# A boundary on eight single PSUM banks, with the next stage's first block product issued inside it

## The chip, the cores and the metric

The kernel runs on one core of a Trainium2 chip. The metric is device time in microseconds of one execution. Engines are called by their work: TensorE multiplies matrices and transposes, VectorE and ScalarE work element by element and read PSUM, GpSimd works on SBUF alone, and SyncE issues the DMAs. The profile's short names are PE, DVE, ACT, POOL and SP.

## The reference

A decoder trunk of two layers over 1024 positions and 1024 channels. A layer has two sub-layers; each is a layer norm of `alpha * x + (1 + gate) * f(x * (1 + scale) + shift)`, with shift, scale and gate from a conditioning vector. The first `f` is a token mixer (a convolution module, differential attention and a spatial gating unit side by side, then one output projection), the second a convolutional feed-forward network:

```python
def conv_ffn(h, w_up, b_up, conv_w, conv_b, w_down, b_down):
    up = causal_dwconv(h @ w_up + b_up, conv_w, conv_b)
    g, val = jnp.split(up, 2, axis=-1)
    return (jax.nn.silu(g) * val) @ w_down + b_down

for l in range(DEPTH):
    ...
    y = jnp.concatenate([y_a, y_b, y_c], axis=-1) @ w_out[l] + b_out[l]
    x = layer_norm(DEEPNORM_ALPHA * x + (1.0 + g1) * y, ln_g[l, 0], ln_b[l, 0])
    h = x * (1.0 + sc2) + sh2
    y = conv_ffn(h, w_up[l], b_up[l], conv_f_w[l], conv_f_b[l], w_down[l], b_down[l])
    x = layer_norm(DEEPNORM_ALPHA * x + (1.0 + g2) * y, ln_g[l, 1], ln_b[l, 1])
```

All is float32. The output projection, the layer norm behind it and the start of `h @ w_up` are the place of this change.

## The kernel before

Positions are held in eight row tiles of 128 (`NT` = 8), channels in eight column tiles of 128. A float32 operand of a matrix product is split into a high part in the matrix format (a ScalarE cast) and a low part (a subtraction, mostly on VectorE); `mm3` (lines 128 to 132) multiplies high by high, high by low and low by high, three matmuls of 128x128 by 128x512 for one product.

*The output projection.* `stage3` (line 891) first runs `out_fill` (line 852), which adds the products of the first head groups into the residual rows `r[t]`, one PSUM bank of 512 columns at a time. Then it opens a new PSUM pool with `self.psum(3, 2)` (three pairs of banks under the name `mm`, two single banks under the name `bank`) and loads and splits the first weights of the up-projection (`up_first`). `boundary` with w = 0 (line 915) runs `out_group` (line 874) for the last two heads: for each row tile, in the order 4, 5, 6, 7, 0, 1, 2, 3, it fills one pair of banks `og` with twelve matmuls and adds its 1024 columns to `r[t]` in one VectorE instruction (line 887).

*The norm and the transposes.* After each row tile `after(t)` runs `ln_rows` (line 348): statistics on VectorE (lines 352, 354, 137), a power on GpSimd (line 138), and the normalisation on ScalarE for tiles 4 to 7 (line 361) or on VectorE for tiles 0 to 3 (line 363); the row is also written to memory. When the later half of the positions (tiles 4 to 7) is normalised, `comb_early` transposes it; when the earlier half (0 to 3) is, `comb_late` does the rest. (In code and text "half" 1 is tiles 4 to 7, and half 0, tiles 0 to 3, comes second in time.) `comb_in` (line 954) takes a bank `tr`, puts four transposes into it, one from each row tile, and has ScalarE scale and shift them into SBUF (line 958). `comb_split` (line 960) casts on ScalarE and subtracts on VectorE (line 962); `tt` in `comb_late` (line 979) adds and subtracts the blocks.

*The up-projection.* `up_phase` (line 1087) multiplies 2x2 blocks with seven products in place of eight; `product(ps, H, n)` (line 1077) is the n-th of them, four blocks k of three matmuls each, from the splits `B11`, `B21`, `B22`, `T1` to `T4` that the boundary made. Product 3 uses `B22` (the later half alone), 1 and 2 use `B11` and `B21` (the earlier half alone), 5, 6, 7 and 4 use `T1`, `T2`, `T3` and `T4`. It is a loop over 22 feature tiles, written out by hand. In the first pass the order on TensorE is 3, 1, 2, 5, 6, 7, then 1 of the next tile, then 4. Product 6 accumulates into the bank of product 1, behind the ScalarE copy `e1` of it (line 1127); product 7 likewise behind the copy `u2` (line 1176). `e1` lies in a page of the tag `Rb`, which has four pages; the boundary's blocks `f` have held all four.

*What sets the order.* Outside `up_phase` a planner orders each engine's queue when the kernel is built: an instruction goes out by its place in the program once its inputs and its tile's memory are free in the planner's own time. Inside `up_phase` the order of TensorE, ScalarE and VectorE is that of the program text. On the chip each queue runs in the order it was given.

Of the kernel before, what the change touches and what calls it, by code (L numbers as in the profile page):

```python
# [17 lines left out]
ALU = mybir.AluOpType  # L18
# [32 lines left out]
class Trunk:  # L51
# [822 lines left out]
    def out_group(self, lhs, w, r, after=None, tiles=range(NT), new=False):  # L874
        nc = self.nc
        for t in tiles:
            ts_ = slice(t * P, (t + 1) * P)
            ps = self.mm("og")
            for n in range(2):
                ns = slice(n * 512, (n + 1) * 512)  # L880
                for k in range(len(lhs)):
                    self.mm3(ps[:, ns], lhs[k][0][:, ts_], lhs[k][1][:, ts_], w[k][0][:, ns], w[k][1][:, ns], k == 0,
                             k == len(lhs) - 1)
            if new:
                nc.scalar.copy(r[t], ps)  # L885
            else:
                nc.vector.tensor_tensor(out=r[t], in0=ps, in1=r[t], op=ALU.add)  # L887
            if after:
                after(t)

    def stage3(self, l, H, O, att):
        nc = self.nc
        att, grow = att
        raws = self.page(H + "a", "wout", shape=(P, 4, 1024))
        for i in range(4 - len(self.woA)):
            self.woA.append(self.scaled_wout(l, KA[len(self.woA)], grow, raws[:, i]))
        wA = [self.split_wout(O, raw) for raw in self.woA]
        ab = None
        if l == 0:
            ab = self.page("rows", "ab")  # L900
            nc.sync.dma_start(ab, self.gab(0, 0, 1))
        order = (4, 5, 0, 1, 2, 3, 6, 7)
        r = {}
        for t in order:
            next(att)
            r[t] = self.load_res(t, ab)
        for _ in att:
            pass
        self.out_fill(self.lhsA, wA, r, order, 1.0 if l else ALPHA)
        self.out_fill(self.lhs0, self.wB[:2], r, order)  # L910
        self.psum(3, 2)
        self.up_first(l, O + "c")
        return r, self.lhsB, self.wB[2:]

# [58 lines left out]
    def comb_late(self, r, H, sc, sh):  # L973
        nc = self.nc
        f = self.parts("Rb", 2, F32) + self.parts("Rb", 2, F32)
        f1, f2, f22 = H["f12"], H["f3"], H["f22"]

        def tt(o, x, y, op):
            nc.vector.tensor_tensor(out=o, in0=x, in1=y, op=op)
        for k in range(4):  # L980
            self.comb_split(H["B22"], k, f22[k], nc.vector)
        for q in range(4):
            self.comb_in(r, 0, q, sc, sh, f[q])
        for q in range(4):
            self.comb_split(H["B11"], q, f[q], nc.vector)
        for q in range(4, 8):
            self.comb_in(r, 0, q, sc, sh, f[q])
        for q in range(4, 8):
            self.comb_split(H["B21"], q - 4, f[q], nc.vector)
        for k in range(4):  # L990
            tt(f2[k], f22[k], f1[k], ALU.subtract)
            tt(f1[k], f1[k], f[k], ALU.subtract)
            self.comb_split(H["T1"], k, f1[k], nc.vector)
        for k in range(4):
            tt(f[k], f2[k], f[k], ALU.add)
            tt(f[4 + k], f[4 + k], f[k], ALU.subtract)
            self.comb_split(H["T2"], k, f[k], nc.vector)
        for k in range(4):
            self.comb_split(H["T3"], k, f2[k], nc.vector)
        for k in range(4):  # L1000
            self.comb_split(H["T4"], k, f[4 + k], nc.vector)
# [85 lines left out]
    def up_phase(self, l, H, A):  # L1087
        nc = self.nc
# [32 lines left out]
                                       in1=u[:, d:], op0=ALU.mult, op1=ALU.add)  # L1121
            tt(u[:, 0:2], u[:, 0:2], self.ffcorr[:, m, :])

        b, d = self.bank("upb"), self.bank("upd")
        self.product(d, H, 3)
        self.product(b, H, 1)
        act.copy(e1, b)
        n11 = n12 = n21 = n22 = o11 = None
        for f in range(NF + 1):
            run, nxt = f < NF, f + 1 < NF  # L1130
            if nxt:
                o22 = n22 if f else None
                k = 2 * ((f + 1) % 2)
# [20 lines left out]
            if run:  # L1154
                d3, d = d, self.bank("upd")
# [45 lines left out]
            if nxt:  # L1201
                b = nb
# [35 lines left out]
    def ffn(self, l, H, A, O):  # L1238
        nc = self.nc
        self.ffn_cols(l)  # L1240
        self.psum(0, 8)
        with self.tc.manual_schedule(engines={nc.tensor.engine, nc.scalar.engine, nc.vector.engine}):
            self.up_phase(l, H, A)
        self.psum(3, 2)
        pages = lambda tag, n: [self.page(tag, "dn", F32R) for _ in range(n)]
        ya, xc = pages(A + "a", 8), pages(O + "c", 4)
        xa = []
        for _ in range(2):
            t = self.page(O + "a", "dn", F32R, (P, 4, 1024))
            xa += [t[:, i] for i in range(4)]  # L1250
        yb, yc = pages(A + "b", 4), pages(A + "c", 4)
        xb = []
        for _ in range(2):
            t = self.page(O + "b", "dn", F32R, (P, 2, 1024))
            xb += [t[:, i] for i in range(2)]
        sets = [(xa[:6], xa[6:] + yb), (ya[:6], yc + ya[6:])]
        grow = self.gate_row(l, 1)
        r = {}
        f0 = 0
        sizes = (2, 3, 3, 3, 3, 3, 2, 3)  # L1260
        for j, n in enumerate(sizes):
            last = j == len(sizes) - 1
            acts, wts = (xb, xc) if j == 0 else sets[j % 2]
            lhs = [self.load_act(l, f0 + i, acts[2 * i], acts[2 * i + 1]) for i in range(n)]
            w = [self.load_wdown(l, f0 + i, wts[2 * i], wts[2 * i + 1], grow) for i in range(n)]
            f0 += n
            if j == 0:
                for t in (4, 5, 6, 7, 0, 1, 2, 3):
                    r[t] = self.page("Ra" if t < 4 else "Rb", "r")
                self.out_group(lhs, w, r, None, (4, 5, 6, 7, 0, 1, 2, 3), True)  # L1270
                self.bg.append(self.residual_in(l, r, O))
                if l + 1 < L:
                    self.mod_tile = [self.page(O + "c", "wada") for _ in range(3)] + [self.page(O + "c", "macc")]
                    self.pump(2)
            elif not last:
                self.out_group(lhs, w, r)
                self.pump(3 * n if l + 1 < L else 2)
            else:
                self.drain_bg()
                if l + 1 < L:  # L1280
                    for ww in range(2):
                        self.affine_cols(l + 1, ww)
                    pre = self.za_first(l + 1, A)
                    Hn = self.boundary(l, 1, lhs, w, r, O)
                    self.bg.append(self.residual(l, r, "tmp"))
                    return Hn, pre
                self.final_rows(l, lhs, w, r)
# [143 lines left out]
```

## Time and profile before

| what | value |
|---|---|
| time, median of 3 runs (lowest to highest) | 2440.98 us (2439.22 to 2441.18) |
| the profiled execution's own time | 2437.79 us |
| its span, first to last instruction | 2436.1 us |
| TensorE busy | 2308.1 us (95%) |
| VectorE busy | 1956.1 us (80%) |
| ScalarE busy | 1049.9 us (43%) |
| granted TensorE clock, mean | 0.974 |
| 1024-column additions of line 887 | 128, mean 1218 ns |

The profile is one execution. Busy time counts an instruction from its start to its end, and successive ones on an engine overlap by a tenth of a microsecond or so; where they queue, the distance from start to start is what one costs. In a row of an engine's order, the bracket is the idle time ahead of it and what ended that. The first layer's boundary lies from about 507 to 571 us of the span and the second's 1201 us later, from about 1708 to 1772.

### The profile page before, as it was taken

To read this page: it belongs to the slowest core of one execution; us is meant where nothing else is said; L and a number is where in the kernel's file an instruction comes from. 1 tells how busy PE (TensorE), PEld (TensorE's weight loads), DVE (VectorE), ACT (ScalarE), POOL (GpSimd) and SP (SyncE) were. 2 spreads that over 40 slices of the span, in tenths; PEclk is the share of its full clock that TensorE was granted. 3 is DMA by queue.
4 is the path that set the end of the run, shared out by engine and by line. 5 is a ranking of instruction groups with operands and counts; after the bars stand their busy time and mean duration, and the time that the engine had idled before them with its cause. 6 is when DMAs were issued, how large, how long until landed. Compare 5 with 4: busy or idle time off the path is not lost.

```text
span 2436.1 us, 28260 instructions
## 1 busy us (share of the span) xinstructions
PE 2308.1 (95%) x10846; PEld 1886.4 (77%) x10846; DVE 1956.1 (80%) x2650; ACT 1049.9 (43%) x1692; POOL 328.9 (13%) x165
## 2 busy tenths in 40 slices
PE   8998999979999999999959999999899999999996
PEld 7787778767888887788848877777688888878885
DVE  7898876778887888877978988657987777797857
ACT  4214754646554555311130257555654555561111
POOL 1143260410000000000020541214100000000003
PEclk9998999999999999999979999999999999999998
DMA  7433462122332333745523244320232222254301
GB/s 294 156 116 120 140 224 104 61 95 90 110 113 88 112 113 121 263 141 179 190 70 117 78 143 160 130 95 27 99 100 87 78 78 87 87 176 169 122 26 69
DMA packets 87672, 294.06 MB, mean 121 GB/s; under 512 B 9265, under 2 KB 18801, under 8 KB 86001
## 3 DMA queue, kind: packets, MB, share of 16 engines
q1 hardware_dynamic: 87536, 292.26, 35.4%
q8 instruction: 85, 1.39, 0.2%
q14 instruction: 51, 0.41, 0.1%
HBM read 228.23 MB, written 64.00 MB: 120 GB/s over the span
## 4 chain that ended last, share of the span: by engine, by line
PE 67%; DVE 17%; issue 6%; ACT 4%; DMA 3%; POOL 2%; SPq 0%; POOLq 0%; DVEq 0%; ACTq 0%
PE upb L1083 6%; PE upb L1084 6%; PE upb L1085 6%; PE og L130 5%; PE og L131 5%; PE og L132 5%; PE sc L733 3%; PE upd L1084 3%; PE upd L1085 3%; PE upd L1083 3%; DVE convacc L410 2%; PE pv L778 2%; PE of L130 2%; PE of L132 2%; PE of L131 2%
## 5 line engine op out<-in xcount | busy, mean ns | idle before, releaser
L1083 PE MATMUL upb<-comb,uw 128*128 128x512 f32 x704 | 274.9, 391 | 9.9 <-DVE upc L1107 5.0
L130 PE MATMUL og<-dn,dn 128*128 128x512 f32 x704 | 275.3, 391 | 2.6 <-ACT r L885 2.1
L131 PE MATMUL og<-dn,dn 128*128 128x512 f32 x704 | 274.5, 390 | 0.0
L132 PE MATMUL og<-dn,dn 128*128 128x512 f32 x704 | 274.3, 390 | 0.0
L1084 PE MATMUL upb<-comb,uw 128*128 128x512 f32 x704 | 274.0, 389 | 0.0
L1085 PE MATMUL upb<-comb,uw 128*128 128x512 f32 x704 | 273.9, 389 | 0.0
L1107 DVE TENSOR_TENSOR uw<-wu,uw 128x512 fp32r<-128x512 f32 x210 | 144.1, 686 | 125.3 <-ACT uw L1110 125.3
L1120 DVE SCALAR_TENSOR_TENSOR cv<-upc,pc,cv 128x1023 f32<-128x1023 f32 (+1 forms) x176 | 225.4, 1280 | 2.9
L138 POOL TENSOR_TENSOR lnrs<-lnrs,mhalf 128x1 f32<-128x1 f32 x32 | 24.8, 779 | 1421.4 <-DVE lnrs L137 1414.9
L887 DVE TENSOR_TENSOR r<-og,r 128x1024 f32<-128x1024 f32 x128 | 155.7, 1218 | 59.0 <-PE og L132 58.4
L410 DVE SCALAR_TENSOR_TENSOR convacc<-convy,pc,convacc 128x1023 f32<-128x1023 f32 (+14 forms) x120 | 176.2, 1469 | 2.3
L125 ACT CAST dn<-actr 128x1024 fp32r<-128x1024 f32 x44 | 46.1, 1049 | 298.1 <-issue 224.4
L1083 PEld LDWEIGHTS upb<-comb,uw 128*128 128x128 f32 x704 | 132.1, 188 | 41.0 <-DVE upc L1107 6.7
L1110 ACT CAST uw<-wu 128x512 fp32r<-128x512 f32 x210 | 121.7, 616 | 83.6 <-DVE wu L1107 77.1
L130 PEld LDWEIGHTS og<-dn,dn 128*128 128x128 f32 x704 | 132.2, 188 | 31.5 <-ACT r L885 3.4
L1085 PEld LDWEIGHTS upb<-comb,uw 128*128 128x128 f32 x704 | 132.2, 188 | 27.5
L132 PEld LDWEIGHTS og<-dn,dn 128*128 128x128 f32 x704 | 132.2, 188 | 27.4
L1084 PEld LDWEIGHTS upb<-comb,uw 128*128 128x128 f32 x704 | 132.2, 188 | 27.2
L131 PEld LDWEIGHTS og<-dn,dn 128*128 128x128 f32 x704 | 132.2, 188 | 26.8
L1083 PE MATMUL upd<-comb,uw 128*128 128x512 f32 x352 | 137.3, 390 | 0.0
L1085 PE MATMUL upd<-comb,uw 128*128 128x512 f32 x352 | 136.9, 389 | 0.0
L1084 PE MATMUL upd<-comb,uw 128*128 128x512 f32 x352 | 136.9, 389 | 0.0
(312 smaller groups left out, 5474.4 us busy)
## 6 DMA issues: line engine op xcount, KB each, us to landing
wada<-in_w_ada SPq DMA_DIRECT2D x96, 512.0 KB, 4.6
wu<-in_w_up_t SPq DMA_DIRECT2D x84, 512.0 KB, 3.6
d_act<-cv SPq DMA_DIRECT2D x44, 512.0 KB, 2.6
actr<-d_act SPq DMA_DIRECT2D x44, 512.0 KB, 4.6
wdn<-in_w_down SPq DMA_DIRECT2D x44, 512.0 KB, 4.2
win<-in_w_fm SPq DMA_DIRECT2D x24, 512.0 KB, 4.0
wtm<-in_w_tm SPq DMA_DIRECT2D x16, 512.0 KB, 3.7
wout<-in_w_out SPq DMA_DIRECT2D x16, 512.0 KB, 6.2
```

Of the source, the lines that this page charges most:

```text
L130: mm(ps, lh, rh, start=first, stop=False)
L131: mm(ps, lh, rl, start=False, stop=False)
L132: mm(ps, ll, rh, start=False, stop=last)
L410: nc.vector.scalar_tensor_tensor(out=acc[:, d:], in0=y[:, :S - d], scalar=w(30 - d), in1=acc[:, d:], op0=ALU.mult, op1=ALU.add)
L733: nc.tensor.matmul(ps[m][:, c0:c1], q[ms, isl], k[ms, c0:c1], start=n == 0, stop=n == 2 and c1 != w)
L887: nc.vector.tensor_tensor(out=r[t], in0=ps, in1=r[t], op=ALU.add)
L1083: mm(ps, w[:, 0, ks], hi[k], start=k == 0 and not more, stop=False, skip_group_check=True)
L1084: mm(ps, w[:, 0, ks], lo[k], start=False, stop=False, skip_group_check=True)
L1085: mm(ps, w[:, 1, ks], hi[k], start=False, stop=k == 3, skip_group_check=True)
L1107: v.tensor_tensor(out=o, in0=x, in1=y, op=op)
L1110: act.copy(self.up_w[n][:, 0], src)
L1120: v.scalar_tensor_tensor(out=u[:, d:], in0=c[:, :S - d], scalar=self.ffw[:, 2 - d, m:m + 1], in1=u[:, d:], op0=ALU.mult, op1=ALU.add)
```

## The change

Three edits. `stage3` opens the pool as eight single banks, `self.psum(0, 8)`, and the feed-forward stage no longer opens one of its own, so that row tiles, transposes and the up-projection's first products draw on the same eight banks. `out_group`, where the pool has no pairs, takes a single bank per half of a row tile and adds it to `r[t]` by itself: two VectorE instructions of 512 columns in place of one of 1024. And `comb_late` takes the bank `upd` and issues product 3 behind the splits of `B22` and ahead of the earlier half's `comb_in` calls, that is, ahead of the transposes that come second in time; `up_phase` uses that bank and no longer issues product 3 itself. The other callers of `out_group` run on pools with pairs and are as before.

```diff
@@ out_group
-            ps = self.mm("og")
+            ps = self.mm("og") if self.psb["mm"] else None
             for n in range(2):
                 ns = slice(n * 512, (n + 1) * 512)
+                po = self.bank("og") if ps is None else ps[:, ns]
                 for k in range(len(lhs)):
-                    self.mm3(ps[:, ns], lhs[k][0][:, ts_], lhs[k][1][:, ts_], w[k][0][:, ns], w[k][1][:, ns], k == 0,
+                    self.mm3(po, lhs[k][0][:, ts_], lhs[k][1][:, ts_], w[k][0][:, ns], w[k][1][:, ns], k == 0,
                              k == len(lhs) - 1)
-            if new:
+                if ps is None:
+                    nc.vector.tensor_tensor(out=r[t][:, ns], in0=po, in1=r[t][:, ns], op=ALU.add)
+            if ps is None:
+                pass
+            elif new:
                 nc.scalar.copy(r[t], ps)
             else:
                 nc.vector.tensor_tensor(out=r[t], in0=ps, in1=r[t], op=ALU.add)
@@ stage3
-        self.psum(3, 2)
+        self.psum(0, 8)
         self.up_first(l, O + "c")
@@ comb_late
         for k in range(4):
             self.comb_split(H["B22"], k, f22[k], nc.vector)
+        self.up_d = self.bank("upd")
+        self.product(self.up_d, H, 3)
         for q in range(4):
             self.comb_in(r, 0, q, sc, sh, f[q])
@@ up_phase
-        b, d = self.bank("upb"), self.bank("upd")
-        self.product(d, H, 3)
+        b, d = self.bank("upb"), self.up_d
         self.product(b, H, 1)
@@ ffn
         self.ffn_cols(l)
-        self.psum(0, 8)
         with self.tc.manual_schedule(engines={nc.tensor.engine, nc.scalar.engine, nc.vector.engine}):
             self.up_phase(l, H, A)
```

## The prediction

> **What bounds the kernel now.** I read the table of stretches first, around the first layer's boundary, to see which engine has no room there; then the order of time on each engine, to see what each waits for; then the chain of waits. Columns of the table: length, then busy time of TensorE, its weight loads, VectorE, ScalarE, GpSimd, with instruction counts, then granted TensorE clock and DMA.
>
> ```profile
> core 0: us, PE busy (x) PEld busy (x) DVE busy (x) ACT busy (x) POOL busy (x), PEclk, DMA share, GB/s
> 510.00:530.00 20.00, 19.97 (x92) 16.19 (x90) 19.30 (x39) 6.05 (x6) 3.27 (x6) 1.00 0.40 156
> 530.00:549.30 19.30, 11.31 (x57) 8.21 (x57) 18.86 (x35) 17.26 (x29) 3.52 (x2) 0.74 0.40 137
> 549.30:560.30 11.00, 11.00 (x50) 9.01 (x48) 11.00 (x20) 9.44 (x19) 0.00 (x0) 0.99 0.00 0
> 560.30:571.20 10.90, 9.07 (x39) 6.64 (x37) 10.87 (x19) 6.37 (x11) 0.00 (x0) 1.00 0.44 147
> 571.20:593.00 21.80, 21.80 (x96) 18.08 (x97) 17.65 (x25) 11.53 (x17) 0.00 (x0) 1.00 0.31 97
> 1711.20:1772.30 61.10, 50.48 (x232) 38.95 (x230) 59.93 (x109) 38.85 (x62) 6.79 (x8) 0.94 0.28 103
> ```
>
> Five rows tell it. From 510.0 to 571.2 VectorE idles 0.70 + 0.44 + 0.00 + 0.03 = 1.17 us of 61.2, while TensorE idles 8 us in the second row alone. From 571.2 on TensorE is full and VectorE has room (17.65 of 21.80). The second layer's boundary, in the last row, is the same: 61.10 - 59.93 = 1.17 us idle. So a boundary is a stretch of VectorE work of 61 us, and TensorE gets its pace back when VectorE has done it. Now TensorE's order of time:
>
> ```profile
> 507.06 0.39 PE L130 MATMUL og<-woh,ybh 128*128 128x512 f32 x1
> ...
> 522.48 0.38 PE L957 MATMUL tr<-ident,r 128*128 128x128 f32 x2
> ...
> 529.59 0.38 PE L957 MATMUL tr<-ident,r 128*128 128x128 f32 x2
> ...
> 541.56 0.69 PE L957 MATMUL tr<-ident,r 128*128 128x128 f32 x2 [3.04 <-DVE r L363]
> 542.90 1.97 PE L957 MATMUL tr<-ident,r 128*128 128x128 f32 x8 [0.66 <-ACT comb L958]
> ...
> 549.27 0.61 PE L1083 MATMUL upd<-comb,uw 128*128 128x512 f32 x1
> 549.72 0.39 PE L1084 MATMUL upd<-comb,uw 128*128 128x512 f32 x1
> ...
> 552.24 0.39 PE L1083 MATMUL upb<-comb,uw 128*128 128x512 f32 x1
> ...
> 554.96 0.39 PE L1083 MATMUL upa<-comb,uw 128*128 128x512 f32 x1
> ...
> 560.89 0.50 PE L1083 MATMUL upb<-comb,uw 128*128 128x512 f32 x1 [0.34 <-ACT upe L1127]
> ...
> 571.16 0.50 PE L1083 MATMUL upb<-comb,uw 128*128 128x512 f32 x1 [0.45 <-DVE upc L1107]
> ```
>
> A product of twelve matmuls takes 554.96 - 552.24 = 2.72 us (a matmul each 0.227 us). The first one, `upd`, starts as the last transposes end. Two waits follow that matter: product 6 for ScalarE's copy `e1` (560.89), product 4 for a VectorE addition (571.16). The chain of waits goes through both:
>
> ```profile
> 558.28 1.90 DVE comb L962 x3
> ...
> 560.25 0.60 ACT upe L1127
> ...
> 560.89 0.50 PE upb L1083
> ...
> 570.51 0.61 DVE upc L1107
> ...
> 571.16 0.50 PE upb L1083
> ```
>
> `e1` is a page of the tag `Rb`, and so are the pages `f` that the last `comb_split` calls read; the copy could not start until VectorE's L962 had let go of one. Both waits hang on VectorE, not on when TensorE began the first product.
>
> **The change part by part.** VectorE's rows for the sum:
>
> ```profile
> 507.59 0.68 DVE L862 SCALAR_TENSOR_TENSOR r<-r,of 128x512 f32<-128x512 f32 x1
> 508.19 0.69 DVE L126 TENSOR_TENSOR uw<-wug,uw 128x512 fp32r<-128x512 f32 x1
> 509.98 1.23 DVE L887 TENSOR_TENSOR r<-og,r 128x1024 f32<-128x1024 f32 x1 [1.11 <-PE og L132]
> ...
> 515.42 1.23 DVE L887 TENSOR_TENSOR r<-og,r 128x1024 f32<-128x1024 f32 x1
> 516.56 0.20 DVE L354 BATCH_NORM_AGGREGATE lnmv<-lnst 128x2 f32<-128x12 f32 x1
> ...
> 519.42 1.28 DVE L352 BATCH_NORM_STATS2 lnst<-r 128x6 f32<-128x512 f32 x2
> ...
> 530.84 1.22 DVE L887 TENSOR_TENSOR r<-og,r 128x1024 f32<-128x1024 f32 x1
> ...
> 540.69 0.81 DVE L363 TENSOR_SCALAR r<-r,lnmv,lnrs 128x1024 f32<-128x1024 f32 x1 [0.44 <-POOL lnrs L138]
> ```
>
> (1) Additions. Eight of 1024 columns go, sixteen of 512 come. Successive instructions overlap, so I take start to start: 1024 columns hold VectorE for 516.56 - 515.42 = 1.14 us, 512 columns from a PSUM bank for 508.19 - 507.59 = 0.60 us. 16 x 0.60 - 8 x 1.14 = +0.48 us per boundary, all of it in the stretch where VectorE has no room.
>
> (2) An earlier first addition. The first half of a row tile is complete 6 x 0.227 = 1.36 us before the second, and can be added in the 1.11 us for which VectorE waits at 509.98. That takes half an addition off the start, 0.54 us. As long as TensorE sets the pace (12 matmuls a row tile, 2.72 us) part of that becomes idle time again: I take -0.3 us, bounds -1.11 and 0.
>
> (3) Product 3 moved. Its twelve matmuls, 2.72 us, leave the place at 549.27 and run before the later half's transposes. Their operands are the splits of `B22`, which VectorE makes ahead of 541; TensorE is idle 3.04 us right there, which covers them. If that cover were gone (`B22` late, or no bank free for `upd`) they would run between the transposes, which wait for ScalarE anyway (0.66 us ahead of the batch at 542.90); at worst they stand where they stand now, so the cost is nil. What is gained? Products 1, 2 and 5 can come up to 2.72 us sooner, and product 6 then meets the wait for `e1` unchanged: 0.34 + 2.72 = 3.06 us of wait instead of 0.34. Late next is exactly what was late before. Worth: 0, bounds -2.72 and 0, taken at 0 because the chain shows VectorE under both waits. No DMA moves with it, and no queue but TensorE's; SyncE's weight loads and GpSimd's powers keep their places.
>
> (4) One pool of eight banks for everything. Before, row tiles had three pairs of their own and the transposes two banks of their own. The rows at 522.48 and 529.59 show that the transposes take their banks early: two banks are begun (x2) between og matmuls, long before the fourth row tile of the half is there, and the last x2 follow 7 us later. With a common pool up to eight banks can be held so, and the row tiles t = 0 to 3, which come behind them, find none until ScalarE empties one. ScalarE's rows say when that can be:
>
> ```profile
> 516.82 1.25 ACT L361 ACTIVATE r<-r,lnnm,lnrs 128x1024 f32<-128x1024 f32 x1 [9.18 <-DVE lnnm L359]
> ...
> 525.21 1.24 ACT L361 ACTIVATE r<-r,lnnm,lnrs 128x1024 f32<-128x1024 f32 x1 [1.70 <-DVE lnnm L359]
> ...
> 530.08 1.44 ACT L958 ACTIVATE comb<-tr,sh,sc 128x512 f32<-128x512 f32 x2
> ```
>
> The fourth tile is normalised at 526.45, so with all j = 3 transposes issued at once the first bank is free at about 527.5 (an estimate: 0.2 us of transposes and 0.72 us, half of the 1.44 us pair, behind 526.45). If transposes begin where they do now (522.48), (522.48 - 507.06) / 0.227 = 68 og matmuls are through, of 96, tiles t = 2 and 3 wait, and og ends at about 527.5 + 4 x 1.36 = 532.9 instead of 529.6. VectorE now runs behind og (its last addition starts at 530.84, over 1 us after og's end at 529.6), so it feels only part: I put 1.0 us of idle time. Against that ScalarE evacuates from 526.7 and not from 530.08, which lets the `B22` splits and the last normalisation follow sooner; the 0.44 us wait for GpSimd may go with it. Net +0.5 us, bounds -0.44 and +6.7 (the second rival).
>
> Sum per boundary: +0.48 - 0.3 + 0 + 0.5 = +0.7 us; two boundaries, +1.4 us. What is gained on VectorE is capped: 1.17 us of idle in 61.2 and 1.11 before it, less 0.48, is 1.8 us per boundary, 3.6 in all, even if nothing at all goes wrong. The profiled execution took 2437.79 us for a span of 2436.1, 3.2 us below the median of 2440.98, so 2437.8 + 1.4 = 2439.2 there and 2442.4 against the median. A difference under 0.2% (4.9 us) is about what a measurement of this kernel can tell from none.
>
> **A rule that speaks against the move.** TensorE's granted clock in stretches of 2 us:
>
> ```profile
> 538.00:540.00 2.00, 0.51 (x4) 0.27 (x3) 2.00 (x5) 1.84 (x4) 1.41 (x1) 0.83 0.75 258
> 540.00:542.00 2.00, 0.44 (x2) 0.29 (x2) 1.56 (x3) 0.30 (x1) 0.65 (x1) 0.50 0.87 266
> 548.00:550.00 2.00, 2.00 (x11) 1.92 (x10) 2.00 (x5) 1.97 (x5) 0.00 (x0) 0.61 0.00 0
> 564.00:566.00 2.00, 1.03 (x4) 0.86 (x5) 2.00 (x4) 1.54 (x3) 0.00 (x0) 1.00 0.89 240
> ```
>
> Around the 3.04 us wait the clock falls to 0.50 and is back only near 549.5; with 2.00 - 1.03 = 0.97 us of idle time (the row from 564) it stays at 1.00. The new wait of 3.06 us before product 6 is as long as the one that lost the clock, though dense matmuls stand before it and sparse transposes before the other. The Trainium skill, TensorE: Matmul & The Clock Gate, section "Part 1: The HAM clock gate", says that the array drops to half clock after an idle window of about 3.4 us and needs about as long of activity to return. By that figure a wait of 3.06 us is too short by itself, and the sum stays 2442.4; the trace here shows the drop at a shorter wait, so it isn't excluded (third rival).
>
> **The rivals.** *TensorE is the bound at the first products, faster.* If the splits of T2 reach their end sooner (other splits, such as T3's, moved behind them), the `e1` wait moves and 2.72 us per boundary comes off whole: 2 x 2.72 = 5.4 below the median, 2435.5 us. For it: TensorE is full from 549.3 to 560.3. Against: the wait at 571.16 stands behind all of VectorE's work, whatever its order, and VectorE can give at most 1.8 us. It decides only if VectorE's stretch ends over 2.45 us sooner, say because og also fills the gaps of out_fill before 507. Chance 0.10.
>
> *The transposes hold the banks, slower.* If they begin when the first tile is ready (518.07, by the first ScalarE row) and og's tile t = 0 must wait until 527.5, og is 9.6 us late; VectorE has the fourth tile's statistics done at 520.7 and nothing else at hand until about 528.5: 7.5 us idle, less 0.8 us got back at the start, 6.7 per boundary. That is 2 x 6.7 = 13.4 us, about 2456; where only t = 2 and 3 wait but VectorE has no filler, 3 us per boundary, 2448. It decides from 2.45 us of lost VectorE time per boundary on. For it: the early transposes at 522.48. Against: og is two thirds through at the place where they begin now. Taken at 2450; chance 0.19.
>
> *The clock falls at the new wait, slower.* At half clock a matmul takes 549.72 - 549.27 = 0.45 us, not 0.227: product 6 costs 12 x 0.22 = 2.7 us more, of which the 0.45 us wait at 571.16 absorbs its part: 2.2 per boundary, which with the +0.7 makes 5.8 us, 2446.8. Against: the wait follows dense work. Chance 0.05.
>
> **How the numbers follow.** No measurable change 0.66 at 2442.4; its own range is 2438 to 2446, from the caps (-1.1 to +2.4 us per boundary). Faster 0.10 at 2435.5, slower 0.19 + 0.05 = 0.24 at 2447 to 2456. The range for 8 in 10 takes in the faster case's price and the lower part of the bank case: 2435 to 2451; what lies outside, mostly the end towards 2456, is about 0.1 to 0.15.
>
> **What would show it.** Right: in the profile after, sixteen additions of 512 columns spaced 0.60 us where they queue; the first product ahead of the last transposes in TensorE's idle time; a wait of about 3 us before product 6 still ended by ScalarE's `e1`; VectorE busy all but 1 to 3 us from 510 to 572; TensorE's last VectorE wait near 571.9. Wrong: product 6 without a wait and TensorE full from some 569 (first rival); og matmuls idle for several us with transposes half done, and VectorE idle at the same time (second); a clock of 0.5 in the row of product 6 (third).

## The result and the profile after

The changed kernel takes 2466.07 us (median of 4 runs, 2464.78 to 2469.1) against 2440.1 us (2437.57 to 2441.18) for the kernel before on the same chip: ratio 1.011, 95% interval 1.0092 to 1.0127. It is 26 us slower, where 2442.4 was forecast, with a range of 2435 to 2451. The profiled executions have spans of 2463.1 and 2436.1 us, 27.0 apart. From the first `og` matmul of a boundary to the last matmul of the up-projection behind it, the traces give 483.03 us after against 471.13 before in the first layer, and 481.11 against 466.90 in the second: +11.9 and +14.2, together 26.1 of the 27.0. The loss lies where the change was made, once per layer.

The table of stretches, from just ahead of the first `og` matmul to the same place of the next feature tile (product 2 of it); first the kernel before, then the changed one with the two stretches in which VectorE stands still. Columns as in the prediction.

```profile
core 0: us, PE busy (x) PEld busy (x) DVE busy (x) ACT busy (x) POOL busy (x), PEclk, DMA share, GB/s
507.00:574.00 67.00, 57.15 (x257) 44.84 (x257) 64.69 (x115) 40.34 (x64) 6.79 (x8) 0.92 0.33 118
```

```profile
506.57:585.50 78.93, 60.50 (x258) 47.66 (x257) 67.18 (x124) 41.64 (x65) 5.34 (x8) 0.87 0.28 100
521.10:525.30 4.20, 3.85 (x23) 3.13 (x24) 0.00 (x1) 3.78 (x6) 0.00 (x0) 1.00 0.62 250
547.90:554.90 7.00, 3.05 (x19) 2.58 (x17) 2.70 (x4) 5.25 (x9) 0.00 (x0) 0.74 0.42 169
```

The stretch grew by 11.9 us. VectorE idled 67.00 - 64.69 = 2.31 us of it before and 78.93 - 67.18 = 11.75 us after; 4.20 us of that stand at 521.10 and 7.00 - 2.70 = 4.30 us at 547.90. TensorE's order of time in the changed kernel tells why. The start of the first `og` matmul is 506.62 after and 507.06 before, so 0.44 us is to be added to a difference of two times.

```profile
506.62 0.39 PE L130 MATMUL og<-woh,ybh 128*128 128x512 f32 x1
...
517.55 1.91 PE L962 MATMUL tr<-ident,r 128*128 128x128 f32 x16
521.24 2.29 PE L962 MATMUL tr<-ident,r 128*128 128x128 f32 x16 [1.77 <-ACT r L361]
523.63 0.50 PE L130 MATMUL og<-woh,ybh 128*128 128x512 f32 x1
...
534.66 0.39 PE L1090 MATMUL upd<-comb,uw 128*128 128x512 f32 x1
...
543.97 1.73 PE L962 MATMUL tr<-ident,r 128*128 128x128 f32 x7 [6.43 <-DVE r L363]
546.15 4.15 PE L962 MATMUL tr<-ident,r 128*128 128x128 f32 x21 [0.45 <-DVE r L363]
...
554.99 0.80 PE L1090 MATMUL upb<-comb,uw 128*128 128x512 f32 x1 [3.85 <-ACT comb L966]
...
575.58 0.50 PE L1090 MATMUL upb<-comb,uw 128*128 128x512 f32 x1 [3.40 <-ACT upe L1182]
...
585.50 0.39 PE L1090 MATMUL upa<-comb,uw 128*128 128x512 f32 x1
```

Sixteen transposes and again sixteen, at four to a bank, are all eight banks. They stand in one piece between the 48th `og` matmul and the 49th: the later half's four row tiles are through, and the row tile t = 0 comes only when the first bank has been emptied. Before, the 49th `og` matmul came 48 x 0.227 = 10.9 us behind the first; here it is 523.63 - 506.62 = 17.0 us, 6.1 us late. What VectorE and ScalarE wait for in that time:

```profile
525.32 0.69 DVE L886 TENSOR_TENSOR r<-og,r 128x512 f32<-128x512 f32 x1 [4.22 <-PE og L132]
...
539.97 0.68 DVE L886 TENSOR_TENSOR r<-og,r 128x512 f32<-128x512 f32 x1
540.57 0.68 DVE L352 BATCH_NORM_STATS2 lnst<-r 128x6 f32<-128x512 f32 x1
...
545.28 2.58 DVE L363 TENSOR_SCALAR r<-r,lnmv,lnrs 128x1024 f32<-128x1024 f32 x3 [0.42 <-POOL lnrs L138]
550.46 2.70 DVE L984 TENSOR_TENSOR comb<-comb,comb 128x512 f32<-128x512 f32 x4 [2.60 <-ACT comb L963]
```

```profile
519.94 2.44 ACT L361 ACTIVATE r<-r,lnnm,lnrs 128x1024 f32<-128x1024 f32 x2 [2.58 <-DVE lnnm L359]
522.80 5.46 ACT L963 ACTIVATE comb<-tr,sh,sc 128x512 f32<-128x512 f32 x8 [0.42 <-PE tr L962]
...
549.65 4.79 ACT L963 ACTIVATE comb<-tr,sh,sc 128x512 f32<-128x512 f32 x7 [14.39 <-PE tr L962]
...
568.52 0.58 ACT L1133 COPY upe<-upb 128x512 f32<-128x512 f32 x1 [0.64 <-DVE comb L967]
...
573.93 0.59 ACT L1169 COPY upe<-upd 128x512 f32<-128x512 f32 x1 [2.75 <-DVE comb L967]
```

The first lines of both are the block itself, the others what follows from it. Three places of the kernel before to set beside them (ScalarE's first emptying of the earlier half's banks; TensorE's product 7 and its next tile):

```profile
542.07 1.45 ACT L958 ACTIVATE comb<-tr,sh,sc 128x512 f32<-128x512 f32 x2 [1.77 <-PE tr L957]
```

```profile
564.97 0.50 PE L1083 MATMUL upb<-comb,uw 128*128 128x512 f32 x1 [1.04 <-ACT upe L1176]
...
574.01 0.39 PE L1083 MATMUL upa<-comb,uw 128*128 128x512 f32 x1
```

The delay grows on its way. The 49th `og` matmul is 6.1 us late. VectorE has the earlier half's last row tile normalised at 545.28 + 2.58 = 547.86, and before at 540.69 + 0.81 = 541.50 (the prediction's row of L363): 6.8 us late. ScalarE begins to empty the earlier half's banks at 549.65 and not at 542.07, 8.0 us late. Of this last step, 1.2 us, the transposes are the reason: those of a row tile go into seven banks side by side (product 3 holds the eighth), so most of the first 28 must be done before the first bank is complete, and they run at half clock (below). ScalarE, which has been idle for 14.39 us by then, empties seven banks in a row, and only then casts. `e1` (568.52, before 560.25) is 8.7 us late, product 7 (575.58, before 564.97) 11.0, and the next tile (585.50, before 574.01) 11.9. The step from 8.7 to 11.0 is the copy L1169, ahead of product 7's `u2` in ScalarE's queue: it waits for VectorE's last `comb_split`, for 2.75 us; in the kernel before the same copy (L1163) waited 0.78 us. The clock, in its column of the table of stretches, falls on top (TensorE idle at full clock first, the transposes and product 1 later at half):

```profile
538.00:540.00 2.00, 0.00 (x0) 0.00 (x0) 2.00 (x6) 0.00 (x0) 0.41 (x1) 1.00 0.00 0
546.00:548.00 2.00, 1.85 (x9) 1.86 (x10) 1.72 (x3) 0.00 (x0) 1.01 (x2) 0.50 0.54 217
556.00:558.00 2.00, 2.00 (x5) 1.32 (x6) 2.00 (x4) 2.00 (x5) 0.00 (x0) 0.50 0.00 0
```

At 0.50 the first matmul of product 1, at 554.99, takes 0.80 us, and the product is drawn out with it.

### The profile page after: what moved, and what is told of

Its sections match the earlier page's. It is cut to its first block, busy times and chain, and to the rows that moved or that the text cites. A ratio compares the mean times of both kernels' runs of the same rounds, so it can differ in the third digit from the quotient of the medians.

```text
span 2463.1 us, 28272 instructions
## 1 busy us (share of the span) xinstructions
PE 2314.9 (94%) x10846; PEld 1890.8 (77%) x10846; DVE 1962.7 (80%) x2666; ACT 1049.7 (43%) x1692; POOL 325.3 (13%) x165
## 4 chain that ended last, share of the span: by engine, by line
PE 67%; DVE 19%; issue 5%; ACT 5%; DMA 3%; POOL 2%; SPq 0%; POOLq 0%; ACTq 0%; DVEq 0%
PE upb L1090 6%; PE upb L1091 6%; PE upb L1092 6%; PE og L130 6%; PE og L131 6%; PE og L132 6%; PE upd L1090 3%; PE upd L1091 3%; PE upd L1092 3%; PE sc L733 3%; DVE convacc L410 2%; PE pv L778 2%; PE of L130 2%; PE of L132 2%; PE of L131 2%
## 5 line engine op out<-in xcount | busy, mean ns | idle before, releaser
L1090 PE MATMUL upb<-comb,uw 128*128 128x512 f32 x704 | 279.1, 397 | 21.4 <-ACT comb L966 7.7
L1091 PE MATMUL upb<-comb,uw 128*128 128x512 f32 x704 | 278.5, 396 | 2.9 <-DVE comb L967 2.9
L1092 PE MATMUL upb<-comb,uw 128*128 128x512 f32 x704 | 277.8, 395 | 0.0
L138 POOL TENSOR_TENSOR lnrs<-lnrs,mhalf 128x1 f32<-128x1 f32 x32 | 22.8, 743 | 1446.1 <-DVE lnrs L137 1431.0
L892 DVE TENSOR_TENSOR r<-og,r 128x1024 f32<-128x1024 f32 x112 | 136.0, 1217 | 55.3 <-PE og L132 55.3
L1090 PEld LDWEIGHTS upb<-comb,uw 128*128 128x128 f32 x704 | 134.4, 191 | 53.0 <-ACT comb L966 8.6
L1091 PEld LDWEIGHTS upb<-comb,uw 128*128 128x128 f32 x704 | 134.3, 191 | 33.7 <-DVE comb L967 6.0
L1092 PEld LDWEIGHTS upb<-comb,uw 128*128 128x128 f32 x704 | 134.4, 191 | 28.0
```

Source lines behind the costliest of these rows:

```text
L1090: mm(ps, w[:, 0, ks], hi[k], start=k == 0 and not more, stop=False, skip_group_check=True)
L1091: mm(ps, w[:, 0, ks], lo[k], start=False, stop=False, skip_group_check=True)
L1092: mm(ps, w[:, 1, ks], hi[k], start=False, stop=k == 3, skip_group_check=True)
```

## The experiments

The theory taken from the trace: the transposes, queued ahead of `og`'s row tiles 0 to 3 in program order, hold the whole common pool while their own inputs are missing, and that is the loss. The rival: product 3, or the bank `upd` that it holds from 534 on, does it, or the half additions do. Stage times in this section run from the first `og` matmul of a boundary to the last matmul of the up-projection behind it, first layer / second layer (before: 471.1 / 466.9). Each comes from one execution.

**Product 3 back in its old place, banks common.** The changed kernel with

```diff
@@ comb_late
-        self.up_d = self.bank("upd")
-        self.product(self.up_d, H, 3)
@@ up_phase
-        b, d = self.bank("upb"), self.up_d
+        b, d = self.bank("upb"), self.bank("upd")
+        self.product(d, H, 3)
```

> The changed kernel with product 3 put back to the start of the up-projection; the pool of eight single banks and the half additions stay. Theory 'banks': the loss comes from the later half's transposes, which take all eight banks while they wait for their last row tiles, so that the matmuls of row tiles 0 to 3 start 6 us late in each boundary; then this kernel is as slow as the changed one, 2460 to 2468 us. Rival 'move': the early product itself (its place in TensorE's queue, its bank) costs the time; then it is back at 2438 to 2444. Rival 'additions': the sixteen half additions and what they displace on VectorE cost it; then 2460 to 2468 too, and e2 tells it from 'banks'.

Measured: 2469.95 us (2467.36 to 2473.45), ratio 1.0118 (1.0102 to 1.0134); stages 484.7 / 480.5. The same block of transposes holds up `og`:

```profile
515.47 1.91 PE L962 MATMUL tr<-ident,r 128*128 128x128 f32 x16
519.15 2.94 PE L962 MATMUL tr<-ident,r 128*128 128x128 f32 x16 [1.77 <-ACT r L361]
521.74 0.78 PE L130 MATMUL og<-woh,ybh 128*128 128x512 f32 x1
...
549.50 0.50 PE L1088 MATMUL upd<-comb,uw 128*128 128x512 f32 x1
```

Product 3 is back behind the transposes (549.50) and nothing is regained: the move is not the cause.

**Two banks for the transposes alone.** The changed kernel with

```diff
-        self.psum(0, 8)
+        self.psum(0, 6, 2)
@@ comb_in
-        pb = self.bank("tr")
+        pb = self.bank("tr", "fill")
```

> The changed kernel with two banks reserved for the boundary's transposes and six single banks for all else, the up-projection included; product 3 stays early, the half additions stay. Theory 'banks': tiles 0 to 3 start without a gap and the time is 2437 to 2445 us, and the first product starts ahead of the last transposes without worth, since product 6 waits for e1 as before. Rival 'move': stays at 2460 to 2468. Rival 'additions': stays at 2460 to 2468.

Measured: 2443.07 us (2437.72 to 2446.58), ratio 1.0007 (0.9998 to 1.0016); stages 473.6 / 471.1. The 26 us between the medians of the common pool and of `before` shrink to less than 3. The transposes again take two banks and trickle in between `og` matmuls; product 3 runs among them (the first rows of each):

```profile
518.34 0.38 PE L962 MATMUL tr<-ident,r 128*128 128x128 f32 x2
...
529.62 0.50 PE L1090 MATMUL upd<-comb,uw 128*128 128x512 f32 x1
...
554.60 0.50 PE L1090 MATMUL upa<-comb,uw 128*128 128x512 f32 x1 [2.45 <-ACT comb L966]
558.03 0.80 PE L1091 MATMUL upa<-comb,uw 128*128 128x512 f32 x1 [2.93 <-DVE comb L967]
```

TensorE got ahead by product 3 and the start of product 1, and the last two rows give it back as waits for the splits; the second of them costs the clock as well (0.80 us).

**The order instead of the banks.** Eight common banks stay, but the later half's transposes are placed behind all row tiles:

```diff
@@ boundary, behind each row tile
-                else:
-                    (self.comb_late if t < 4 else self.comb_early)(r, H, sc, sh)
+                elif t < 4:
+                    self.comb_early(r, H, sc, sh)
+                    self.comb_late(r, H, sc, sh)
```

> The changed kernel with the later half's transposes placed behind all eight row tiles in the program, so that they can't take a bank ahead of one; eight common banks, early product and half additions stay. Theory 'banks': the 6 us gap in TensorE's row tiles is gone (12 us in all), while the earlier half's transposes still fill eight banks side by side and ScalarE still gets its first one late: 2444 to 2458 us. Rivals 'move' and 'additions': 2460 to 2468.

Measured: 2444.87 us (2443.1 to 2446.54), ratio 1.0017 (1.0008 to 1.0026); stages 474.0 / 472.5. This separates the parts of the loss. The banks are as common as in the changed kernel, the earlier half's transposes still run side by side (ScalarE empties seven of their banks in a row there too, from 544.45), and the waits that they bring are still there:

```profile
549.80 0.80 PE L1091 MATMUL upb<-comb,uw 128*128 128x512 f32 x1 [3.86 <-ACT comb L967]
554.92 0.80 PE L1092 MATMUL upb<-comb,uw 128*128 128x512 f32 x1 [1.36 <-DVE comb L968]
```

But `og` runs through (its 96 matmuls stand in one piece from 510.30 to 532.1), and the stages come down from +11.9 / +14.2 to +2.9 / +5.6. So some 9 us per boundary are the blocked row tiles, and the long waits further down (3.86 us here, 3.85 in the changed kernel's row for the same place) cost only what is left.

**Product 3 late, with two banks for the transposes.** The second experiment with product 3 issued in `up_phase` again, by the same edit as in the first.

> As e2, with product 3 put back to the start of the up-projection. The difference e3 - e2 is what the move alone is worth. Theory 'VectorE sets the pace of the boundary' (the prediction's): within 2 us of e2, both 2437 to 2445. Rival 'TensorE would be the bound': e2 is 5.4 us faster than e3. Rival 'move costs': e3 2438 to 2444, e2 well above.

Measured: 2442.85 us, ratio 1.0011 (1.0002 to 1.002); stages 474.4 / 469.0. It did not test what it was meant to: since both stages now share a pool, the twelve matmuls were still let through early, between the transposes, from 533.48 to 540.39. So the pool was opened anew in front of the up-projection, as the kernel before does:

```diff
@@ ffn
         self.ffn_cols(l)
+        self.psum(0, 8)
```

> As e3, with the pool of eight opened anew ahead of the up-projection, as in the kernel before. In e3's trace product 3 still ran between the transposes, though the program text has it behind them: with one pool nothing held it back. Here it can't start until the boundary is through, so e5 against e2 is the move alone, on the same two-bank transposes and half additions. Theory 'VectorE sets the pace': within 2 us of e2 (2443), 2438 to 2445. Rival 'TensorE would be the bound': e2's gain is lost, 2448 or more. Rival 'the move costs': 2436 to 2440.

Measured: 2439.04 us (2435.91 to 2442.68), ratio 0.9995 (0.9986 to 1.0004); stages 470.9 / 468.6. Product 3 stands at 549.36, behind the transposes. Of the change only the sixteen half additions are left, and they cost nothing that can be told. Against the second experiment the late product is 4 us faster by the medians; the two intervals overlap (0.9998 and 1.0004), so a loss from the early product is likely there but not shown.

**Product 3 early, on the pools of before as far as they allow it.** The kernel before with a bank for `upd` alone, for which `og` gives up one pair of banks and the up-projection keeps seven:

```diff
@@ stage3, with a fourth number for a pool of one bank
-        self.psum(3, 2)
+        self.psum(2, 2, 0, 1)
@@ comb_late
+        self.up_d = self.one.tile([P, 512], F32, tag="one", name=self.nm("upd"), bufs=1)
+        self.product(self.up_d, H, 3)
@@ ffn
-        self.psum(0, 8)
+        self.psum(0, 7)
```

> The kernel before (row tiles on pairs, additions of 1024 columns, two banks for the transposes) with product 3 issued early into a bank of its own; one pair of the row tiles is given up for it, and the up-projection has seven banks beside it. Theory 'VectorE sets the pace': no gain, 2438 to 2444 us. Rival 'TensorE would be the bound': 2 x 2.72 us off, about 2435. Rival 'the move costs': 2446 or more.

Measured: 2449.53 us (2447.62 to 2453.49), ratio 1.004 (1.0027 to 1.0052). TensorE's row at product 6, and two half microseconds ahead of it in the table of stretches:

```profile
560.26 0.80 PE L1093 MATMUL upb<-comb,uw 128*128 128x512 f32 x1 [2.85 <-ACT upe L1136]
```

```profile
559.00:559.50 0.50, 0.00 (x0) 0.00 (x0) 0.50 (x2) 0.00 (x0) 0.00 (x0) 1.00 0.00 0
559.50:560.00 0.50, 0.00 (x0) 0.00 (x0) 0.50 (x2) 0.37 (x1) 0.00 (x0) 0.63 0.00 0
```

The 2.72 us come back as a wait of 2.85 us for `e1`, as the prediction had it, and the clock falls in that wait. The boundary stages are only 472.5 / 468.2, +1.4 / +1.3; most of the 9 us lies elsewhere (the stretch behind the second up-projection alone is 5.9 us longer). By its total the rival that the move costs (2446 or more) came out and not the theory; but `og` has a pair less here and the up-projection a bank less, and the time was lost mostly where the move is not. The boundary's share is what this run shows; its total is not a price of the move.

**VectorE's room, tried from the other side.** If VectorE sets the boundary, taking work off it must help. Twice from the kernel before: the low parts of `T3` on GpSimd, and the row tiles 0 to 3 normalised on ScalarE.

```diff
@@ comb_late (first kernel)
-            self.comb_split(H["T3"], k, f2[k], nc.vector)
+            self.comb_split(H["T3"], k, f2[k], nc.gpsimd)
@@ boundary (second kernel)
-            self.ln_rows(r[t], w == 0 and t >= 4)
+            self.ln_rows(r[t], w == 0)
```

> The kernel before, with the four subtractions for the low part of T3 on GpSimd in place of VectorE: 4 x 0.60 us per boundary off VectorE, onto an engine that is idle there (some 1.3 us each by half of its 1024-column rows). Theory 'VectorE sets the pace of the boundary': up to 2 x 2.4 = 4.8 us faster, 2435.5 to 2439; if product 7 then waits for GpSimd, less. Rival 'TensorE or ScalarE is the bound': no change, 2440 within 2.

> The kernel before, with row tiles 0 to 3 of the first boundary of each layer normalised on ScalarE, as tiles 4 to 7 are, in place of VectorE: 4 x 0.72 us per boundary off VectorE, 4 x 1.15 us onto ScalarE. Theory 'VectorE alone sets the pace': up to 5.5 us faster, 2435 to 2439. Rival 'ScalarE is as tight between 530 and 558': the casts and evacuations come later by what is added, no gain or a loss, 2440 to 2447.

Measured: GpSimd 2449.99 us (2446.32 to 2451.54), ratio 1.0039 (1.0026 to 1.0051), a clear miss; ScalarE 2438.84 us (2436.44 to 2440.94), ratio 0.999 (0.9981 to 0.9999), 0.1% faster, with 1 just outside the interval. The ScalarE kernel's stages are 471.8 / 469.1, so its boundary is not shorter than before (471.1 / 466.9), and the 0.1% does not come from there: taking work off VectorE gained nothing at the place where it was taken. With GpSimd the wait for the earlier half's first row tile grew instead of shrinking (3.04 us before), and the stages were 473.3 / 469.7:

```profile
543.76 0.69 PE L957 MATMUL tr<-ident,r 128*128 128x128 f32 x2 [4.60 <-DVE r L363]
```

The trace shows why the wait grew: GpSimd begins the first of the subtractions at 539.03, it takes 2.39 us (1.6 on average, where 1.3 was expected), and the power for row tile 3 (L138) comes behind it, at 541.38; the normalisation of that tile starts only at 541.95 and takes 1.75 us. The boundary accounts for about 5 us of the loss and other stages for the rest.

**Both together.** The half additions on single banks (the reopened pool above) with the normalisation on ScalarE:

> The changed kernel with three things altered: two banks of their own for the transposes, product 3 back in the up-projection's phase (with the pool reopened in front of it), and the row tiles 0 to 3 of the boundary normalised on ScalarE. So of the change only the sixteen half additions on single banks are left, beside the move of the normalisation. If the small effects of the runs before add (0.9995 for the half additions alone, 0.999 for ScalarE's normalisation alone): 2436 to 2440 us, ratio 0.9985. VectorE is then 4 x 0.8 us freer per boundary and the wait of the later half of the transposes for r[3] should fall from about 3 us. Rival: both gains are spread of the other stages, which the planner orders anew for every kernel; then 2437 to 2445 and no measurable change.

Measured: 2440.53 us (2436.32 to 2443.95), ratio 1.0 (0.9991 to 1.0009); stages 471.1 / 468.3, against 470.9 / 468.6 without the move of the normalisation. The small gains do not add. VectorE has less to do and idles as much more:

```profile
505.41:572.41 67.00, 56.16 (x258) 43.60 (x258) 63.25 (x123) 44.40 (x68) 4.36 (x8) 0.95 0.33 118
530.00:560.00 30.00, 21.38 (x99) 15.78 (x100) 27.17 (x48) 28.59 (x49) 0.54 (x1) 0.89 0.25 88
```

Over the same 67 us VectorE is busy 63.25 us and no longer 64.69, ScalarE 44.40 and no longer 40.34; and from 530 to 560 it is ScalarE that is all but full (28.59 of 30.00, before 26.65), with VectorE idle for 2.83 us behind it. No version tried here beats the kernel before by more than 0.1%.

| kernel | us | ratio to the kernel before (95%) |
|---|---|---|
| common pool, product 3 early (the change) | 2466.07 | 1.011 (1.0092 to 1.0127) |
| common pool, product 3 late | 2469.95 | 1.0118 (1.0102 to 1.0134) |
| transposes on two banks, product 3 early | 2443.07 | 1.0007 (0.9998 to 1.0016) |
| transposes on two banks, product 3 late | 2439.04 | 0.9995 (0.9986 to 1.0004) |
| common pool, product 3 early, transposes behind all row tiles | 2444.87 | 1.0017 (1.0008 to 1.0026) |

## Why the prediction was wrong, step by step

*What bounds the kernel* held for this change. Of the 11.9 us that the changed kernel's stretch grew, 11.75 - 2.31 = 9.4 are VectorE's idle time. It does not hold the other way round: with four normalisations off VectorE the stages did not get shorter, and in the last experiment ScalarE is then all but full from 530 to 560. VectorE is not the only bound there.

*Step (1), the additions*, held. In the changed kernel a queued half addition holds VectorE for 540.57 - 539.97 = 0.60 us, the figure used, and with everything else undone the total is 2439.04 us. *Step (2)*, the earlier first addition, was a third of a microsecond and no run tells it apart.

*Step (3), product 3*, held in its mechanism. (Its "later half's transposes" are those that come second in time, of the row tiles 0 to 3.) Where it runs ahead and the banks are not the question, the gain is a wait again: 2.85 us at `e1` in the kernel with the move alone (3.06 were worked out), 2.45 and 2.93 us at the splits in the kernel with two banks. What the value 0 left out is the fallen clock behind the new wait. In the list of waits, too, one was passed over, the longest of the three in that stretch: 1.04 us ahead of product 7 (564.97). By the medians the early product is 3.9 us faster than the late one with a common pool, where the transposes have delayed everything, and 4.0 us slower with two banks for the transposes; in both pairs the intervals overlap.

*Step (4), one pool of eight banks*, failed. It was put at +0.5 us per boundary with an upper bound of +6.7; the boundary lost 11.9 and 14.2 us, of which the order experiment gives some 9 (9.0 and 8.6) to this step. Two things went wrong in it.

First, the choice between the ends. The step took the place of the first transposes from the trace of before (522.48, 68 `og` matmuls through) and concluded that only the row tiles t = 2 and 3 would wait. But that place belonged to the old pool and its queue: with two banks only two transposes per row tile could be issued ahead of time, and `og` passed the rest. It is not even fixed with two banks: in the second experiment the first pair stands behind 55 `og` matmuls, (518.34 - 505.87) / 0.227. The program has the transposes in front of row tile 0, and with banks for all of them they were issued in front of it: 48 matmuls are through, not 68. The second rival had the mechanism and the place, all banks held and t = 0 waiting; it was given 0.19 because of that borrowed place. Its estimate of the block was too high (9.6 us; measured 6.1, since ScalarE had the fourth tile normalised at 519.94 + 2.44 = 522.4 and not 526.45; by the two times that it names, 518.07 and 527.5, it would be 9.4, and the gap from 520.7 to 528.5 is 7.8 us, not 7.5).

Second, the upper bound of 6.7 us ended the account where `og` resumes. The block itself cost VectorE 4.22 us of idle time, less than the 7.5 in that bound; the rest of the loss lay behind it. Not in the account were the earlier half's transposes side by side (1.2 us more of lateness, and VectorE idle for another 4.30 us from 547.90 on), the clock at 0.50 in that stretch, and the copy L1169 ahead of `u2`, by which a lateness of 8.7 us becomes 11.0. All were visible as questions in the trace of before: who is next when this is late. They were asked for product 3 and not for the banks. They don't simply add: in the order experiment the same waits stand, at about 3 to 6 us per boundary in all, product 3's share included.

*The clock.* The third rival's event, a drop at the wait ahead of product 6, came true in the kernel with the move alone: the wait is 2.85 us and the matmul behind it takes 0.80 us. The rule quoted from the Trainium skill (TensorE: Matmul & The Clock Gate, "Part 1: The HAM clock gate"), an idle window of about 3.4 us, would have left the clock up there; the trace has it falling between 559.5 and 560.0, some 2.2 us after the last matmul ended, and in the changed kernel still at 1.00 from 538 to 540 and down only after 542, some 5 us after TensorE fell idle. The page also says that the window runs free of the kernel; that makes the scatter plausible, but a drop after 2.2 us is short of a whole idle window, so here the measurement decides.

## What to carry to other kernels

Where work that is still waiting for its inputs takes buffers from the same pool as work that is ready, and stands ahead of it in program order, more buffers can make it worse: here two banks kept the transposes from running ahead of `og`, eight let them take everything. Before merging pools, count for each user how many buffers it can take before its last input is there, and read the order from the program, not from a trace in which the old pool size enforced it. The Trainium skill (Perfetto Trace Analysis, "Matmul Optimizations") advises using all eight PSUM banks; the common pool and the six and two banks of the second experiment both use all eight, and 23 us lie between them (2466.07 and 2443.07), in who may hold which.

## What the runs showed of the hardware

Behind a run of matmuls the granted clock fell to 0.50 some 2.2 us (the kernel with the move alone) and some 5 us (the changed kernel) after TensorE's last one. Behind sparse work it fell sooner: some 1.8 us after the changed kernel's last transposes, which end at 551.14 (its clock from 552 to 554 is 0.74 on average), and some 0.6 us after a single matmul between two waits in the kernel with two banks, which ends at 555.10 (0.72 from 555.5 to 556.0). So a wait of 2 to 3 us in front of a product must be counted with a chance of half speed behind it (0.80 us for the first matmul, not 0.50).

Kernels that differ in one stage differ by several microseconds in stages whose code is the same: from the last matmul of the first up-projection to the first `og` matmul of the second boundary it is 730.0 us before and 737.8 us in the kernel with the low parts of `T3` on GpSimd, though its edit is not in that stretch. The planner orders the queues anew for every kernel; that this is the reason was not tested. Small differences of totals were therefore read beside the stage's own time.
